# The first norm's modulation, cut from halves into quarters

## The chip, the cores and the metric

The kernel runs on one core of a Trainium2 chip. The metric is the device time of one execution in microseconds (us). A core has engines that run side by side, each through its own list of instructions in a fixed order: PE (matmuls; PEld is its weight load), DVE and POOL (vector work), ACT (activations, also copies), SP (here only DMA issue). DMA queues move data between HBM and the on-chip memory SBUF; PE writes to PSUM.

## The reference

Two layers of a diffusion backbone work on 512 latent tokens and 256 context tokens of width 1024, in 32-bit floats. What matters here is the start of layer 0:

```
def rmsnorm(x, g):
    y = xf * lax.rsqrt(jnp.mean(xf * xf, axis=-1, keepdims=True) + NORM_EPS)
    return (y * g.astype(jnp.float32)).astype(x.dtype)

def modulate(h, shift, scale):
    return h * (1 + scale) + shift
...
aq_x, bq_x, ak_x, av_x, bk_x, bv_x = jnp.split(h_x @ w_in, cuts, axis=-1)
```

`shift` and `scale` are products of a conditioning vector with a weight matrix `ada_w`: the latent tokens have one vector (`c`), the context tokens another (`c_ctx`), with the same weights. The modulated `h` then goes into a wide projection. Its first unit is two heads' K and Q and a block of V; attention on them follows, while the next unit is projected. The rest of the kernel (attention, output projection, feed-forward, layer 1) is the same in both versions.

## The kernel before

Activations lie with the feature on the partitions: `xr[k]`, k = 0 to 7, is the latent x of features 128k to 128k+127, a tile of 128 x 512; `cr[k]` is the context's, 128 x 256. `hb[k]` holds the modulated h of tile k in two parts, a rounded high part and the low rest, for latents (`hx`) and context (`hc`). A weight tile too is split: `wh` by a cast on ACT, `wl` by a subtraction on DVE. Each product is three matmuls: high x high, high weight x low h, low weight x high h.

The start of layer 0 (function `add_ada0` and the block below it) runs like this. `ada_w` for shift and scale is loaded in two halves `b`, of eight 512 KB tiles each (128 rows, 512 columns of shift and of scale). `ada0_mm(b)` multiplies them on PE with the conditioning columns, in four groups of 32 columns of the array side by side, into the PSUM tile `t`. `ada0_h(b)` copies the sums (`ada_acc`, DVE), turns them by PE transposes, adds the bias (`mod`) and makes 1 + scale times the gain (`amod`), and then makes h for four feature tiles: `h_make` multiplies x by `amod` and by x's 1/rms `ns_y` into `ns_h` (DVE), adds the shift into the high part (ACT), and makes the low part (DVE).

`part(range(4))` then runs the products of feature tiles 0 to 3 for K, Q (PSUM tiles `lin`, 512 columns) and V (`s`, 256 columns); the context's rms and its tiles 0 to 3 are made behind it in program order; the second half of the modulation follows, `part(range(4, 8))`, and context tiles 4 to 7. `keep_busy` puts matmuls of no use on PE, in waits. Behind the block, `qk_x` applies rope to K and Q (DVE and POOL) and evacuates them, `qk_c` and `v_group` project the context, and the attention steps begin; K's halves are swapped by a DMA (`k<-k`), which the second of each pair of score matmuls needs.

The code's order is not the engines' order. Tiles come from pools with a set number of buffers; a scheduler orders each engine's instructions by its own model of time, unless `tc.issue_after` sets an instruction behind another. `Stream` (`S`) holds the weight loads in order; `request` issues DMAs ahead, `next` makes the split and hands out the tile. At most eight SP loads are under way: each waits for the one eight before it on its semaphore.

## Time and profile before

| | |
|---|---|
| median of 3 runs | 1638.08 us (1630.61 to 1639.51) |
| the profiled execution, its own time | 1638.05 us |
| its span, first to last instruction | 1636.2 us |
| busy PE / DVE / ACT / POOL | 96% / 77% / 46% / 17% |
| granted clock of PE | 0.991 |
| first modulation matmul; first product | 12.94 us; 26.60 us |
| last K and Q product of latents starts | 57.76 us |
| first attention score | 79.75 us |

A row of the profile in order of time gives the start, the duration, the engine, the line of the kernel, the operation, out<-in by the program's names, the shape and a count; in brackets stands how long the engine was idle before it, and what ended that. Matmuls are pipelined, so that a row is longer than the distance to the next. In rows of stretches, the columns stand in the order that the text names.

### The profile page before, as it was taken

The numbers are of one execution on the slowest core, as the hardware profiler recorded it, in microseconds if no ns is written. First come the engines' busy times: TensorE is split into PE (matmuls) and PEld (weight loads), VectorE is DVE, ScalarE is ACT, GpSimd is POOL, SyncE is SP. The second block draws the span as 40 slices with busy tenths as digits, with TensorE's granted clock in tenths as the row PEclk, the third lists the DMA queues.
The fourth block names the chain that finished last, engine by engine and source line by source line (L and its number), as shares of the span: only waits on it lengthen the run. The fifth ranks groups of instructions, "written<-read, shape, count | busy, mean of one in ns | idle before, by whom it ended". The sixth has DMA issues, their size and how long they took to land.

```text
span 1636.2 us, 26336 instructions
## 1 busy us (share of the span) xinstructions
PE 1569.7 (96%) x10222; PEld 1404.1 (86%) x10222; DVE 1255.7 (77%) x2156; ACT 747.8 (46%) x1325; POOL 271.1 (17%) x312
## 2 busy tenths in 40 slices
PE   5999998999999899999999999999999999999997
PEld 3798987877878899999999998887788899989897
DVE  4757698976597788979898877787665987869686
ACT  4446554556344433432424254455654542524344
POOL 2222222345010000010100011264322000000001
PEclk9999999999999999999999999999999999999999
DMA  9312244544235365576766752311010442323321
GB/s 342 99 57 87 87 158 125 185 136 133 68 116 158 94 180 162 143 203 170 192 181 166 210 141 90 104 52 39 14 40 15 156 136 69 122 86 104 116 78 52
DMA packets 69364, 199.00 MB, mean 122 GB/s; under 512 B 6916, under 2 KB 19364, under 8 KB 69240
## 3 DMA queue, kind: packets, MB, share of 16 engines
q1 hardware_dynamic: 59464, 164.40, 31.2%
q0 software_dynamic: 9200, 32.39, 9.3%
q8 instruction: 81, 1.33, 0.3%
q10 hardware_dynamic: 576, 0.52, 0.1%
q14 instruction: 43, 0.35, 0.1%
HBM read 160.45 MB, written 4.86 MB: 101 GB/s over the span
## 4 chain that ended last, share of the span: by engine, by line
PE 62%; DVE 8%; DMA 4%; issue 4%; ACT 2%; POOL 0%; DVEq 0%; SPq 0%; ACTq 0%; POOLq 0%
PE f L1274 4%; PE f L1272 4%; PE f L1273 4%; PE f L1685 4%; PE f L1684 4%; PE f L1683 4%; PE f L1314 3%; PE f L1313 3%; PE f L1315 3%; PE t L1517 2%; PE lin L207 2%; PE lin L208 2%; PE lin L209 2%; DMA wl<-raw 2%; PE f L1736 2%
## 5 line engine op out<-in xcount | busy, mean ns | idle before, releaser
L196 ACT ACTIVATE wh<-raw 128x1024 fp32r<-128x1024 f32 (+1 forms) x95 | 91.2, 976 | 227.8 <-DVE raw L507 100.8
L207 PE MATMUL lin<-hb,wh 128*128 128x512 f32 (+1 forms) x456 | 163.1, 358 | 7.5 <-DVE q L372 2.2
L208 PE MATMUL lin<-hb,wh 128*128 128x512 f32 (+1 forms) x456 | 160.4, 352 | 0.1
L209 PE MATMUL lin<-hb,wl 128*128 128x512 f32 (+1 forms) x456 | 159.1, 349 | 0.0
L197 DVE TENSOR_TENSOR wl<-raw,wh 128x1024 fp32r<-128x1024 f32 (+1 forms) x95 | 105.9, 1121 | 36.3 <-ACT wh L196 34.2
L269 DVE SCALAR_TENSOR_TENSOR junk<-raw,tables 128x1024 bf16<-128x1024 f32 x80 | 98.4, 1230 | 16.8 <-DMA raw<-in_ada_wT_dram 16.4
L202 POOL DMA_DIRECT2D wl<-raw x40 | 34.9, 873 | 449.4 <-ACT wl L201 405.0
L207 PEld LDWEIGHTS lin<-hb,wh 128*128 128x128 f32 x456 | 86.6, 190 | 22.2 <-issue 4.3
L1313 PE MATMUL f<-g,wh 128*128 128x256 f32 (+1 forms) x304 | 102.7, 339 | 0.8 <-DVE s L1302 0.6
L1314 PE MATMUL f<-g,wh 128*128 128x256 f32 (+1 forms) x304 | 102.7, 339 | 0.0
L1684 PE MATMUL f<-hb,wh 128*128 128x256 f32 x360 | 101.7, 283 | 0.0
L1272 PE MATMUL f<-hb,wh 128*128 128x384 f32 x288 | 97.4, 338 | 4.4 <-ACT q L1259 4.4
L1683 PE MATMUL f<-hb,wh 128*128 128x256 f32 x360 | 101.4, 283 | 0.0
L1685 PE MATMUL f<-hb,wl 128*128 128x256 f32 x360 | 101.2, 283 | 0.0
L1315 PE MATMUL f<-g,wl 128*128 128x256 f32 (+1 forms) x304 | 100.6, 336 | 0.0
L158 ACT CAST wh<-raw 128x1024 fp32r<-128x1024 f32 x61 | 63.9, 1048 | 78.6 <-PE lin L208 24.5
L1274 PE MATMUL f<-hb,wl 128*128 128x384 f32 x288 | 97.2, 338 | 1.0 <-DMA wl<-raw 1.0
L1273 PE MATMUL f<-hb,wh 128*128 128x384 f32 x288 | 97.2, 337 | 0.0
L208 PEld LDWEIGHTS lin<-hb,wh 128*128 128x128 f32 x456 | 86.8, 190 | 11.5 <-issue 0.9
L159 DVE TENSOR_TENSOR wl<-raw,wh 128x1024 fp32r<-128x1024 f32 x61 | 79.3, 1301 | 22.2 <-ACT wh L158 22.1
L209 PEld LDWEIGHTS lin<-hb,wl 128*128 128x128 f32 x456 | 86.7, 190 | 10.5 <-issue 0.3
L339 POOL TENSOR_TENSOR ns_a<-ns_a,ns_s 128x256 f32<-128x256 f32 (+1 forms) x16 | 18.9, 1178 | 435.3 <-ACT ns_s L335 426.5
(395 smaller groups left out, 4952.6 us busy)
## 6 DMA issues: line engine op xcount, KB each, us to landing
raw<-in_w_dram SPq DMA_DIRECT2D x132, 512.0 KB, 3.6
raw<-in_ada_wT_dram SPq DMA_DIRECT2D x80, 512.0 KB, 3.8
wl<-raw POOLq DMA_DIRECT2D x40, 512.0 KB, 5.8
raw<-in_w_ab_dram SPq DMA_DIRECT2D x24, 512.0 KB, 4.1
raw<-in_ada_w_dram SPq DMA_DIRECT2D x16, 512.0 KB, 9.5
k<-k SPq DMA_DIRECT2D x16, 384.0 KB, 5.9
raw<-in_w_c_dram SPq DMA_DIRECT2D x12, 512.0 KB, 3.9
nb<-in_na_bias_dram POOLq DMA_DIRECT2D x16, 256.0 KB, 3.6
```

What stands on the lines that cost most here:

```text
L207: nc.tensor.matmul(ps, wh(k), xh(k), start=k == 0, stop=False)
L208: nc.tensor.matmul(ps, wh(k), xl(k), start=False, stop=False)
L209: end = nc.tensor.matmul(ps, wl(k), xh(k), start=False, stop=k == n - 1)
L1272: nc.tensor.matmul(ps, wh(k), b[:, 0, :], start=k == 0, stop=False)
L1273: nc.tensor.matmul(ps, wh(k), b[:, 1, :], start=False, stop=False)
L1274: nc.tensor.matmul(ps, wl(k), b[:, 0, :], start=False, stop=k == 3)
L1313: nc.tensor.matmul(ps, hi, g[:, 0, cols[v]], start=first, stop=False)
L1314: nc.tensor.matmul(ps, hi, g[:, 1, cols[v]], start=False, stop=False)
L1315: nc.tensor.matmul(ps, lo, g[:, 0, cols[v]], start=False, stop=last)
L1683: nc.tensor.matmul(ps, wh(k), b[:, 0, :], start=k == 0, stop=False)
L1684: nc.tensor.matmul(ps, wh(k), b[:, 1, :], start=False, stop=False)
L1685: nc.tensor.matmul(ps, wl(k), b[:, 0, :], start=False, stop=k == 3)
```

## The change

- `ada_w` for the first norm comes in quarters of two feature tiles. A buffer of 512 KB holds two row blocks (128 x 2 x 256 each) and is loaded by two DMAs of 256 KB. SP's first 43 DMAs are chained, so that they go in the written order; the conditioning row `crow` is loaded second, not after x.
- Per quarter there are 32 modulation matmuls of 128 columns (before, 32 of 256 for each half), one transpose, two adds and one scale.
- x/rms is made ahead by DVE (`scaled`, tiles `xn`), in buffers borrowed from the attention's pools (`Places`). h is then made by two ACT passes with the scale and the shift as operands (the high part, and a 32-bit copy) and one DVE subtraction, in place of DVE, ACT, DVE.
- The products run by feature tile: K and Q of tile k (`part_kq`), V of tile k (`part_v`). Between them stand the next quarter's modulation matmuls, half behind `part_v(k)`, half behind `part_kq(k + 1)`; `queued` fixes this.
- The context's rms comes in the last quarter, and all eight context tiles are made behind the last modulation.
- PE begins with 44 `keep_busy` matmuls; 20 stand behind the first quarter (before: 10 and 9 behind the two halves' transposes).
- The weight splits of the first unit are queued behind named instructions (`pins`); those of the second V half lie in a pool of their own.

```diff
+        def start(self, dst, src):
+            with queued(*(self.chain or [])[-1:]):
+                dma = nc.sync.dma_start(dst, src)
...
     def ada_mm(ps, raw, k, first, last):
         for j in range(4):
-            nc.tensor.matmul(
-                ps[32 * j : 32 * j + 32, 0:256], csil[:, k, :], raw[:, j * 256 : (j + 1) * 256], start=first, stop=last
-            )
...
+            end = nc.tensor.matmul(ps[32 * j : 32 * j + 32, 0:P], csil[:, k, :], raw[:, j * P : (j + 1) * P], start=first, stop=last)
+        return end
...
+            S.pools["ada"] = s0.enter_context(tc.tile_pool(name="p0_ada", bufs=6, reuse_waits="tile"))
...
+            keep_busy(psk, 44)
...
+            def ada0_h(b, ps):
+                sb = p0.tile([P, P], F32, tag="ada_acc", name="ada_acc", bufs=2)
+                nc.vector.tensor_copy(sb, ps[:, 0:P])
+                made = ada_out(sb, tp, 2 * b)
+                if b == 0:
+                    scaled((2, 3), made)
+                ends = []
+                for k in (2 * b, 2 * b + 1):
+                    t = p0.tile([P, NX], F32, tag="ns_h", name="ns_h", bufs=2)
+                    for z in (hx[k][:, 0, :], t):
+                        act = nc.scalar.activation(z, xn[k], AF.Identity, bias=mod[0][:, 0, 0, k : k + 1], scale=amod[0][:, 0, 0, k : k + 1])
+                    ends.append((act, nc.vector.tensor_sub(hx[k][:, 1, :], t, f32(hx[k][:, 0, :]))))
+                if b == 0:
+                    scaled(range(4, KT), ends[1][1])
+                return made, ends
...
+            ps = tp()
+            end = ada0_mm(ps, range(4), 16)
+            rx = rstd_of(tp(), sq_sum(xr, px, apart=True), D, px)
+            keep_busy(psk, 20, end)
+            root = rms_made[-1]
+            scaled(range(2))
+            made, ends = ada0_h(0, ps)
+            pins.extend([(root, made), (ends[0][0], ends[0][1]), ends[1]])
...
-            part(range(4))
-            rc = rstd_of(tp(), sq_sum(cr, p0), D, p1)
-            for k in range(4):
-                h_make(k, hc[k], cr[k], rc, 0, 0, 1, p0)
-            ada0_h(1, ada0_mm(1))
-            keep_busy(tp(), 9)
-            wv.append(tuple(wslice(t, 256) for t in S.next()))
-            part(range(4, KT))
-            for k in range(4, KT):
-                h_make(k, hc[k], cr[k], rc, 0, 0, 1, p0)
...
+            for b in range(1, 4):
+                k = 2 * b - 2
+                ps = tp()
+                part_kq(k)
+                ada0_mm(ps, range(2), (16, 20, 22)[b - 1], part_v(k))
+                end = ada0_mm(ps, range(2, 4), (16, 20, 22)[b - 1], part_kq(k + 1))
...
+                if b == 3:
+                    with queued(*c_pins, end):
+                        rc = rstd_of(tp(), sq_sum(cr, pc_), D, pc_)
+                part_v(k + 1)
+                _, ends = ada0_h(b, ps)
...
+            ctx_h(range(4))
+            part_kq(KT - 2)
+            part_kq(KT - 1)
+            part_v(KT - 2)
+            part_v(KT - 1)
+            ctx_h(range(4, KT))
```

What the engines get, at the places that matter. First DVE before, from the last step of x's rms (`ns_y`) to the last weight split of K, Q and V:

```order
L321 SCALAR_TENSOR_TENSOR ns_y<-ns_t,ns_y 128x512
L649 COPY ada_acc<-t 128x256
L249 TENSOR_TENSOR mod_116<-t,adab 128x2x2 x4
L257 SCALAR_TENSOR_TENSOR amod_118<-mod_116,ng 128x2x4
L353 SCALAR_TENSOR_TENSOR ns_h<-res,amod_118,ns_y 128x512 x2
L159 TENSOR_TENSOR wl<-raw,wh 128x1024
L341 TENSOR_TENSOR ns_a<-ns_a,ns_s 128x256
L355 SCALAR_TENSOR_TENSOR hb_124<-ns_h,mod_116,hb_124 128x512
L355 SCALAR_TENSOR_TENSOR hb_125<-ns_h,mod_116,hb_125 128x512
L341 TENSOR_TENSOR ns_a<-ns_a,ns_s 128x256
L353 SCALAR_TENSOR_TENSOR ns_h<-res,amod_118,ns_y 128x512
L159 TENSOR_TENSOR wl<-raw,wh 128x1024
```

And DVE after, over the same stretch (the borrowed buffers are called `scratch`; L738 is x/rms, L218 the weight split, L729 the low part):

```order
L350 SCALAR_TENSOR_TENSOR scratch<-scratch 128x512
L738 TENSOR_TENSOR scratch<-res,scratch 128x512 x2
L266 TENSOR_TENSOR mod_117<-t,adab 128x2x2 x2
L273 SCALAR_TENSOR_TENSOR amod_119<-mod_117,ng 128x2x2
L738 TENSOR_TENSOR scratch<-res,scratch 128x512 x2
L218 TENSOR_TENSOR wl<-raw,wh 128x1024
L729 TENSOR_TENSOR hb_124<-ns_h,hb_124 128x512
L729 TENSOR_TENSOR hb_125<-ns_h,hb_125 128x512
L738 TENSOR_TENSOR scratch<-res,scratch 128x512 x4
L218 TENSOR_TENSOR wl<-raw,wh 128x1024 x2
```

The x/rms of all eight tiles now stands ahead of the second and third weight split, and the context's sums are gone from here.

On PE, the turn-around from one modulation to the products that use it; before, at the second half (L235 modulation, L243 transposes, L219 fillers, L667 to L669 K and Q):

```order
L677 MATMUL s<-wl,hb_127 128x256
L235 MATMUL t<-raw,craw 32x256 x28
L243 MATMUL t<-ident,ada_acc 128x128 x2
L219 MATMUL t<-ones,ident 128x128 x9
L667 MATMUL lin<-hb_128,wh 128x512 x2
L668 MATMUL lin<-hb_128,wh 128x512
```

After, on PE at the second quarter's turn-around (L771 the last V product of tile 1, L262 the transpose, L759 to L761 K and Q, L769 V):

```order
L771 MATMUL s<-wl,hb_125 128x256
L262 MATMUL t<-ident,ada_acc 128x128
L759 MATMUL lin<-hb_126,wh 128x512 x2
L769 MATMUL s<-wh,hb_126 128x256 x2
L760 MATMUL lin<-hb_126,wh 128x512
L761 MATMUL lin<-hb_126,wl 128x512
```

There are three such places now; the modulation matmuls have moved ahead between the products, and no filler stands behind the transpose.

On PE, where the context's products end and the scores begin, before (L399 to L401 the context's V, L804 and L805 scores):

```order
L399 MATMUL lin<-wh,hb_131 128x256
L400 MATMUL lin<-wh,hb_131 128x256
L401 MATMUL lin<-wl,hb_131 128x256
L804 MATMUL s<-k_630,q 128x256
L805 MATMUL s<-k_631,q 128x256
```

And after (L229 and L230 the context's Q, L917 the first score, L428 the first of the context's V):

```order
L229 MATMUL lin<-hb_131,wh 128x256
L230 MATMUL lin<-hb_131,wl 128x256
L917 MATMUL s<-k_755,q 128x256
L428 MATMUL lin<-wh,hb_124 128x256
L429 MATMUL lin<-wh,hb_124 128x256
```

The first score has moved ahead of the context's V, and V's second half no longer lies behind the context's K and Q.

## The prediction

> **What bounds the kernel now.** I read the page's head first, then busy times by stretch, since the change touches only the start, then the start's instructions in order of time.

> ```profile
> span 1636.2 us, 26336 instructions
> ```

> ```profile
> 0.00:74.00 74.00, 52.30 (x371) 38.47 (x372) 45.09 (x84) 33.74 (x57) 22.00 (x28) 0.95 0.66 233
> 74.00:1637.00 1563.00, 1517.43 (x9854) 1365.63 (x9852) 1210.58 (x2072) 714.05 (x1268) 249.10 (x284) 0.99 0.40 116
> ```

> The columns are the stretch, its length, busy time (and instructions) of PE, PEld, DVE, ACT and POOL, the granted clock, the DMA share and GB/s. Behind 74 us PE works 97% of the time, so a delay at the start is a delay at the end unless a later wait takes it up. Before it PE stands 21.7 us. I measure the change by one mark, the first attention score with all projections of the first unit done: 79.75 us.

> ```profile
> 12.94 1.08 PE L235 MATMUL t<-raw,craw 128*32 128x256 f32 x8 [12.94 <-DMA raw<-in_ada_w_dram]
> ...
> 15.67 3.78 PE L312 MATMUL t<-ns_a,ones 128*128 128x512 f32 x4 [0.37 <-DVE ns_a L341]
> ...
> 19.38 2.37 PE L235 MATMUL t<-raw,craw 128*32 128x256 f32 x40
> ...
> 22.34 0.64 PE L235 MATMUL t<-raw,craw 128*32 128x256 f32 x8 [0.60 <-DMA raw<-in_ada_w_dram]
> ...
> 23.87 2.40 PE L219 MATMUL t<-ones,ident 128*128 128x128 f32 x20
> ...
> 26.60 0.50 PE L667 MATMUL lin<-hb,wh 128*128 128x512 f32 x1 [0.34 <-ACT hb L354]
> ...
> 28.81 0.50 PE L668 MATMUL lin<-hb,wh 128*128 128x512 f32 x1 [1.70 <-DVE hb L355]
> ...
> 73.99 0.28 PE L399 MATMUL lin<-wh,hb 128*128 128x256 f32 x1
> ...
> 79.75 0.28 PE L804 MATMUL s<-k,q 128*128 128x256 f32 x1
> ```

> A 32-bit matmul leaves two records, so x8 is four matmuls. The modulation of tiles 0 to 3 waits for its weights until 22.34; the first product (K of tile 0) runs at 26.60, and the next waits 1.70 us for the low half on DVE. From 73.99 to 79.75 run the 48 products of the context's V, 0.12 us each; those of 512 columns I take at twice that, 0.24.

> **The change part by part.** The sum is made on the profiled execution: 1638.05 us, of which 1.85 lie around the span; the median of the three runs is 1638.08.

> *To the first product.* PE now begins with 44 filler matmuls. The row at 23.87 gives ten in 2.40 us, 0.24 each. They can begin when the identity is made, at 3.5 us (POOL row below). At full rate throughout they end at 14, at half rate throughout at 24.6. In the trace PE is at half rate from 12.94 (1.08 us for what takes 0.64 at 22.34) through the sums at 15.67 and at full rate at 19.38, some 6 us later with gaps in between. I take 5 us at half rate: they end at 16.4.

> ```profile
> 3.18 0.31 POOL masks.py:199 TENSOR_SCALAR_AFFINE_SELECT ident<-ident 128x128 f32<-128x128 f32 x1
> ...
> 22.25 0.69 DVE L321 SCALAR_TENSOR_TENSOR ns_y<-ns_t,ns_y 128x512 f32<-128x512 f32 x1
> ...
> 24.47 0.17 DVE L257 SCALAR_TENSOR_TENSOR amod<-mod,ng 128x8 f32<-128x8 f32 x1
> ...
> 25.84 1.32 ACT L354 ACTIVATE hb<-ns_h,mod 128x512 fp32r<-128x512 f32 x2
> 26.01 1.22 DVE L159 TENSOR_TENSOR wl<-raw,wh 128x1024 fp32r<-128x1024 f32 x1
> ```

> ```profile
> 1091.38 1.09 PE L1517 MATMUL t<-pt,gv 128*64 128x128 f32 x16
> ```

> A quarter's modulation is 32 matmuls, 64 records of 128 columns in place of 256. With 256 columns and 32-wide weights a record takes 2.37/40, 0.056 without the tail. L1517 has 128 columns on 64-wide weights, two groups of the array side by side, and takes 0.055 a record (16 in 1.09, tail off), half of the full-width filler's 0.11. So time goes with columns and width, and I take 0.028: 2.0 us a quarter with the tail. The upper end is 0.056, 3.7 us, since no row shows a quicker matmul. The first quarter ends at 18.4. The sums of squares are three matmuls now, at full rate half of the 1.89 that each took at 15.67: 21.3. From their end to x's rms it was 3.5 us (19.45 to 22.94): 24.8. Two x/rms products (0.69 each, as at 22.25), two of the adds and the scale (0.35), one ACT pass (0.66): the first product at 27.4, 0.8 later than before. The smaller first load buys nothing, because PE is late, not the DMA. The 20 fillers end at 26.1, beside the rms.

> *Pair 0.* Behind the scale, at 26.6, DVE's order has two x/rms (1.4), a weight split (1.22), two low halves (1.4), four x/rms (2.8) and two splits (2.44): V's low weights come at 35.9. Eight V products are left on PE, and the 64 records of quarter 1 stand behind them: 38.9. PE idles behind its first product as it did at 28.81, and then the clock was halved:

> ```profile
> 30.00:32.00 2.00, 1.51 (x4) 0.66 (x2) 2.00 (x3) 1.13 (x2) 2.00 (x1) 0.50 1.04 386
> ```

> Most of that falls where DVE is late anyway; I add 0.6 (bounds 0 and 3): 39.5.

> *Turn-around and period of a quarter.* From the last record of a quarter: 12 V products (1.44), a transpose (0.4), adds and scale (0.35), one ACT pass (0.66), hops (0.2): 3.0. No filler or other product is left to put there, so PE idles 1.2 us of it. Then 4 products on the high half (0.7), 0.7 of waiting for the second ACT pass and the subtraction, and 14 products and the next quarter's records: 4 x 0.24 + 10 x 0.12 + 1.0 + 6 x 0.24 + 1.0 = 5.6. So a quarter takes 10.0, and tiles 2, 4 and 6 reach PE at 42.5, 52.5 and, with the context's sums (two matmuls of 256 columns, 0.95, and their wait), 63.5. Before, there was one turn-around behind the first. The DMAs are not late: a buffer for quarter 2 comes free when quarter 1's first tile is read, at some 38, and is needed at 47; loads of that size, x's, took 6.0 us to land:

> ```profile
> res<-in_xT_dram SPq DMA_DIRECT2D x8, 256.0 KB, 6.0
> ```

> *The tail.* The last pair has 36 products, 5.8, and 0.7 of waiting: 70. The context's K and Q (48 x 0.12) would end at 75.8, but their tiles are now all made last on DVE, where four of eight stood at 42.84 beside PE's work:

> ```profile
> 42.84 0.88 DVE L353 SCALAR_TENSOR_TENSOR ns_h<-res,amod,ns_y 128x256 f32<-128x256 f32 x2
> ...
> 59.35 2.33 DVE L353 SCALAR_TENSOR_TENSOR ns_h<-res,amod,ns_y 128x256 f32<-128x256 f32 x2
> ...
> 64.00 2.33 DVE L372 SCALAR_TENSOR_TENSOR k<-rbuf,k 64x512 fp32r<-64x512 f32 x2
> 66.36 2.21 DVE L159 TENSOR_TENSOR wl<-raw,wh 128x1024 fp32r<-128x1024 f32 x1
> ```

> From 64.2 DVE has two low halves (1.4), eight context tiles (8 x 0.9), four rope operations (2.8) and the K and Q low parts (2.8): 78.4. Beside POOL's rope work the same shapes took 1.45, about 0.95 and 0.99 us more (59.35 to 66.36), 3.4 in all; I take 2 (bounds 0 and 3.4): 80.4, and PE ends K and Q 0.5 later. Then one cast (1.05), one split (1.22) and K's context low part (0.88) stand ahead of the first score, which PE's order now has ahead of the V products: 84.1. Then 48 V products, 5.8: 89.9 in place of 79.75. Before, the second V half, 48 products, lay over that evacuation; now it is spent. Costed at nothing: x/rms itself (one DVE pass replaces one, ACT's 8 extra passes of 0.66 are in the turn-around), the earlier table load (hidden before the x tiles), lambda's few small operations (beside quarter 2's products).

> The sum is 10 us: 1648.

> [...] The row at 28.81 shows the clock halved after a gap of 1.70 us. [...]

> **The rivals.**

> *Modulation at 0.056, or half clock in each turn-around.* The first costs 1.7 us in each of four quarters: 7, so 1655. The second costs some 3.5 us in three turn-arounds: 1658. [...]

> *The delay is taken up later (not slower).* The order also shifts in the heads of about 240 to 440 us, where PE stands:

> ```profile
> 220.00:240.00 20.00, 17.78 (x114) 15.48 (x113) 19.12 (x30) 10.86 (x23) 4.03 (x2) 1.00 0.38 128
> 240.00:260.00 20.00, 16.16 (x95) 12.94 (x93) 17.45 (x31) 11.40 (x25) 2.72 (x2) 1.00 0.37 120
> ```

> If the new order closed these 6.1 us, 1642; with the like behind them, 1636. It decides from 2 us on, where the loss falls under 8. Against it: DVE is 87 to 96% busy there, and gets no less work.

> *Faster.* If DVE kept ahead of PE, the products (24 us), three quarters (6), sums (1) and the context (12) from 27.4 on would end at 70, ten before 79.75: 1628. Against it stands DVE's order in pair 0 and in the tail.

> **How the numbers follow.** The forecast (1643 to 1653) gets 0.5, the dearer cases 0.2, the delay taken up 0.19, faster 0.11. A measurement of this kernel tells about 0.5%, 8 us, from no change: of the forecast 0.1 lies under 8, so slower 0.6, same 0.29, faster 0.11. The range runs from 1634, into the case taken up, to 1661, past the dearer ones; the forecast's own is 1643 to 1653.

> **What the profile after would show.** First product at 27 to 28; a modulation record at 0.028; PE waiting twice at each of three turn-arounds; the first score waiting on DVE's K part, ahead of the context's V; that V ending near 90; PE's idle before 90 over 21 us. I am wrong if that V ends before 82, or if it ends near 90 and the span is not 6 us longer.

## The result, and the profile after

The changed kernel takes 1663.49 us (median of four runs, 1658.61 to 1666.81) against 1637.27 for the kernel before: ratio 1.0168, interval 1.0141 to 1.0194. It is 26 us slower. The forecast was slower by 10, with a range up to 1661: the sign was right, the time lies outside. The profiled execution, the longest of the four, took 1666.81 us; 1.81 of them lie around its span. A second set of five runs gave 1659.4 us against 1633.33, ratio 1.0153 (1.0133 to 1.0174).

The page's head, then busy times by stretch (columns as in the prediction):

```profile
span 1665.0 us, 26804 instructions
```

```profile
0.00:74.00 74.00, 58.41 (x543) 48.85 (x544) 30.84 (x67) 32.34 (x51) 10.37 (x19) 0.95 0.66 219
74.00:1665.00 1591.00, 1533.57 (x9900) 1377.63 (x9899) 1224.62 (x2093) 721.38 (x1282) 255.83 (x294) 0.99 0.40 115
```

The first row misleads: PE is busier there than before (58.41 against 52.30 us), but 64 filler matmuls are in it, against 19 before. The second stretch is 28 us longer than before, so most of the loss shows only behind 74 us. The start in order of time on PE (L240 and L238 fillers, L256 modulation, L341 sums, L262 transpose, L759 and L760 K of tile 0):

```profile
11.83 4.18 PE L240 MATMUL lin<-ones,ident 128*128 128x128 f32 x36
15.94 1.52 PE L256 MATMUL t<-raw,craw 128*32 128x128 f32 x48
17.96 0.43 PE L256 MATMUL t<-raw,craw 128*32 128x128 f32 x8 [0.49 <-DMA raw<-in_ada_w_dram]
20.57 0.43 PE L256 MATMUL t<-raw,craw 128*32 128x128 f32 x8 [2.19 <-DMA raw<-in_ada_w_dram]
20.92 2.84 PE L341 MATMUL t<-scratch,ones 128*128 128x512 f32 x6
23.60 4.63 PE L238 MATMUL lin<-ones,ident 128*128 128x128 f32 x40
28.07 0.27 PE L262 MATMUL t<-ident,ada_acc 128*128 128x128 f32 x1
29.83 0.50 PE L759 MATMUL lin<-hb,wh 128*128 128x512 f32 x1 [1.50 <-ACT hb L728]
31.92 0.50 PE L760 MATMUL lin<-hb,wh 128*128 128x512 f32 x1 [1.59 <-DVE hb L729]
```

The fillers end at 16.0, close to the forecast 16.4, and PE then waits for the last loads until 20.57: the DMA was late, not PE. Since the sums stand behind the modulation, the whole rms follows that load. The three turn-arounds:

```profile
43.56 0.73 PE L759 MATMUL lin<-hb,wh 128*128 128x512 f32 x2 [1.36 <-ACT hb L728]
45.00 0.50 PE L760 MATMUL lin<-hb,wh 128*128 128x512 f32 x1 [0.47 <-DVE hb L729]
54.08 0.73 PE L759 MATMUL lin<-hb,wh 128*128 128x512 f32 x2 [1.36 <-ACT hb L728]
55.51 0.50 PE L760 MATMUL lin<-hb,wh 128*128 128x512 f32 x1 [0.47 <-DVE hb L729]
66.96 0.73 PE L759 MATMUL lin<-hb,wh 128*128 128x512 f32 x2 [1.37 <-ACT hb L728]
68.39 0.50 PE L760 MATMUL lin<-hb,wh 128*128 128x512 f32 x1 [0.47 <-DVE hb L729]
```

Two waits at each, of the size forecast. The end of the start, first DVE's list, then PE (L229 the context's Q, L917 and L918 scores, L428 to L430 the context's V), then the clock by stretches:

```profile
78.03 1.16 DVE L382 SCALAR_TENSOR_TENSOR ns_h<-res,amod,scratch 128x256 f32<-128x256 f32 x1
79.11 1.51 DVE L384 SCALAR_TENSOR_TENSOR hb<-ns_h,mod,hb 128x256 fp32r<-128x256 f32 x1
...
84.45 0.48 DVE L384 SCALAR_TENSOR_TENSOR hb<-ns_h,mod,hb 128x256 fp32r<-128x256 f32 x1
86.68 1.23 DVE L171 TENSOR_TENSOR wl<-raw,wh 128x1024 fp32r<-128x1024 f32 x1 [1.75 <-ACT wh L170]
87.94 0.87 DVE L401 SCALAR_TENSOR_TENSOR k<-lin,k 64x256 fp32r<-64x256 f32 x2
```

```profile
83.03 0.39 PE L229 MATMUL lin<-hb,wh 128*128 128x256 f32 x1 [1.37 <-DVE hb L384]
...
84.99 0.58 PE L229 MATMUL lin<-hb,wh 128*128 128x256 f32 x1 [0.79 <-DVE hb L384]
...
88.41 0.58 PE L917 MATMUL s<-k,q 128*128 128x256 f32 x1 [2.20 <-DVE k L401]
88.96 0.55 PE L428 MATMUL lin<-wh,hb 128*128 128x256 f32 x1
89.31 0.41 PE L429 MATMUL lin<-wh,hb 128*128 128x256 f32 x1
...
96.83 0.28 PE L430 MATMUL lin<-wl,hb 128*128 128x256 f32 x1
97.32 0.39 PE L918 MATMUL s<-k,q 128*128 128x256 f32 x1 [0.21 <-DMA k<-k]
```

```profile
83.70:88.40 4.70, 1.72 (x7) 1.13 (x5) 2.83 (x5) 3.13 (x5) 0.00 (x0) 0.50 0.00 0
90.00:94.00 4.00, 4.00 (x21) 4.00 (x21) 0.91 (x3) 0.00 (x0) 0.00 (x0) 0.51 1.02 232
```

PE waits for DVE's context tiles; behind these waits of 0.3 to 1.4 us the clock is at half from 83.7 on, so already ahead of the longest wait, the 2.20 us for K's low part (the L229 row at 84.99 takes 0.58, the one at 83.03 0.39). The context's V then runs at 0.21 us a product until 94 and at 0.12 behind that. The second score row stands at 97.32, where before it stood at 79.87.

How the delay of one instruction grows, each time against the same instruction of the kernel before (start times; the lines are those of before):

| instruction, and its time before | after | delay |
|---|---|---|
| first product, 26.60 | 29.83 | 3.2 |
| second score row (L805), 79.87 | 97.32 | 17.5 |
| first context scores (L769), 119.49 | 137.05 | 17.6 |
| last context attention (L852), 287.88 | 302.02 | 14.1 |
| last head's V products (L982), 444.69 | 469.20 | 24.5 |
| first feed-forward product (L1272), 557.12 | 586.17 | 29.1 |
| end of the span, 1636.2 | 1665.0 | 28.8 |

So there are two losses: 17.5 us in the start, and some 7 from 119 to 445 us, where only the order of the engines differs. What follows behind 445 us scatters. In the second profile of the same kernel the delays at 119 us, at 445 us and at the end were 19.0, 24.4 and 17.0: the wait of 6.64 us ahead of the first feed-forward product, shown further down, was not there.

### The profile page after: what moved, and what is told of

Read it like the earlier page. It is cut to its first block, busy times and chain, and to the rows that moved or that the text cites. A ratio compares the mean times of both kernels' runs of the same rounds, so it can differ in the third digit from the quotient of the medians.

```text
span 1665.0 us, 26804 instructions
## 1 busy us (share of the span) xinstructions
PE 1592.0 (96%) x10442; PEld 1426.5 (86%) x10442; DVE 1255.5 (75%) x2159; ACT 753.7 (45%) x1333; POOL 266.2 (16%) x312
## 4 chain that ended last, share of the span: by engine, by line
PE 51%; DVE 6%; DMA 5%; issue 5%; ACT 2%; POOL 0%; DVEq 0%; POOLq 0%; ACTq 0%; SPq 0%
PE f L1799 4%; PE f L1798 4%; PE f L1797 4%; DMA wl<-raw 3%; PE f L1388 3%; PE f L1386 3%; PE f L1387 3%; PE f L1428 3%; PE f L1427 3%; PE f L1429 3%; PE t L1631 2%; PE f L1851 2%; PE f L1852 2%; PE f L1850 2%; PE t L1617 2%
## 5 line engine op out<-in xcount | busy, mean ns | idle before, releaser
L217 ACT ACTIVATE wh<-raw 128x1024 fp32r<-128x1024 f32 (+1 forms) x99 | 95.2, 979 | 232.1 <-DVE raw L536 124.5
L229 PE MATMUL lin<-hb,wh 128*128 128x512 f32 (+1 forms) x456 | 161.4, 354 | 3.9 <-DVE hb L384 3.6
L230 PE MATMUL lin<-hb,wl 128*128 128x512 f32 (+1 forms) x456 | 160.1, 351 | 0.0
L218 DVE TENSOR_TENSOR wl<-raw,wh 128x1024 fp32r<-128x1024 f32 (+1 forms) x99 | 110.4, 1122 | 35.2 <-ACT wh L217 32.9
L228 PEld LDWEIGHTS lin<-hb,wh 128*128 128x128 f32 x456 | 87.0, 192 | 23.5 <-issue 7.8
L229 PEld LDWEIGHTS lin<-hb,wh 128*128 128x128 f32 x456 | 87.2, 191 | 16.8 <-DVE hb L384 4.7
L1388 PE MATMUL f<-hb,wl 128*128 128x384 f32 x288 | 97.5, 338 | 0.1
L230 PEld LDWEIGHTS lin<-hb,wl 128*128 128x128 f32 x456 | 87.1, 191 | 10.8 <-issue 0.7
L170 ACT CAST wh<-raw 128x1024 fp32r<-128x1024 f32 x57 | 59.7, 1047 | 79.4 <-PE lin L229 25.9
L171 DVE TENSOR_TENSOR wl<-raw,wh 128x1024 fp32r<-128x1024 f32 x57 | 73.7, 1294 | 25.6 <-ACT wh L170 25.3
L368 POOL TENSOR_TENSOR ns_a<-ns_a,ns_s 128x256 f32<-128x256 f32 (+1 forms) x12 | 12.4, 1037 | 427.1 <-ACT ns_s L364 420.5
## 6 DMA issues: line engine op xcount, KB each, us to landing
raw<-in_ada_w_dram SPq DMA_DIRECT2D x32, 256.0 KB, 5.7
nb<-in_na_bias_dram POOLq DMA_DIRECT2D x16, 256.0 KB, 3.3
```

The source lines that it names most:

```text
L228: nc.tensor.matmul(ps, wh(k), xh(k), start=k == 0, stop=False)
L229: nc.tensor.matmul(ps, wh(k), xl(k), start=False, stop=False)
L230: end = nc.tensor.matmul(ps, wl(k), xh(k), start=False, stop=k == n - 1)
L1388: nc.tensor.matmul(ps, wl(k), b[:, 0, :], start=False, stop=k == 3)
```

## The experiments

Each kernel was timed beside the kernel before, whose median was then 1632.67 to 1633.58 us. They ran on four chips, so between kernels of different rounds the ratios, with their 95% intervals, are the safer comparison. The base of most is the changed kernel with 52 fillers, the first one below. The delay at the first context scores (119.49 us before) and at the last head's V (444.69) is given as in the table, against the profile of before. That profile is itself some 1 to 1.7 us late there: in the four kernels that alter it only further on, the row at 59.49 us came 1.0 to 1.7 us earlier.

**The order between 240 and 440 us.** The scheduler's order there flips with a few fillers. So four fillers can give the kernel before the order of after, and eight can give the changed kernel the order of before, with nothing else moved.

```diff
-            keep_busy(psk, 44)
+            keep_busy(psk, 52)
```

> The changed kernel with 52 instead of 44 fillers ahead of the first modulation. The eight more end some 1.9 us later, still before the last load of the first quarter (20.57 us), so the start should stand as it is; but with them the order of the engines between 240 and 440 us is that of the kernel before. Theory O (the changed order between 240 and 440 us costs the 7 us by which the offset grows there): about 7 us less than the changed kernel, 1656.5. Rival D (the order costs nothing; a late start is what makes those stages wait longer): 1663, within 2 us.

```diff
-        ps = linp().rearrange("p (t c) -> p t c", t=2)
+        ps = linp()
+        keep_busy(ps, 4, c_end[0])
+        ps = ps.rearrange("p (t c) -> p t c", t=2)
         v_group(ps, 0, wv)
```

`c_end` is the last product of the context's Q. With four fillers the order of after results on PE, row for row, with 80 that of before, with six a third.

> The kernel before with four fillers (0.24 us each) ahead of the context's V. They alone make the order between 240 and 440 us that of the changed kernel, row for row. Theory O: 1 us for the fillers and 7 for the order, 1645. Rival D: 1 us for the fillers, 1638.

> The kernel before with 80 fillers at that place, some 19 us of pure delay of PE, as much as the changed kernel is late at its first scores (17.5 us); the order between 240 and 440 us stays that of the kernel before. Theory O: the delay goes through to the end one for one, 1655 to 1657. Rival D: it grows on the way as in the changed kernel (17.5 to 26), 1664. A third way, that later waits take part of it up: below 1650.

> The kernel before with six fillers (1.4 us) at that place: a third order between 240 and 440 us, unlike both. Theory O: 1639 for the fillers alone, and by the order some us more or less, of unknown sign; a time below 1637 would be a better order than both. Rival D: 1638.5, within 2 us.

> The changed kernel as it is, on the chip on which the variants ran, as a reference for them and for the waits behind 440 us. Theory O (the order between 240 and 440 us costs 4 to 7 us): 1660 to 1664, that is 4 to 7 us over the kernel with 52 fillers (1656.6). Rival D: 1656 to 1658, the same as that kernel. Behind 440 us, if the wait of the last output-projection load (2 us) belongs to this start, it shows again at 2 us; if it is chance, at 0.8 to 1.2.

| kernel | median, us | ratio (interval) | delay at 119 / 445 us |
|---|---|---|---|
| after, again | 1659.4 | 1.0153 (1.0133 to 1.0174) | 19.0 / 24.4 |
| after, 52 fillers | 1656.63 | 1.0138 (1.0123 to 1.0154) | 17.7 / 18.8 |
| before, 4 fillers | 1638.16 | 1.0021 (1.0007 to 1.0034) | -0.3 / 3.7 |
| before, 6 fillers | 1635.89 | 1.0009 (0.9994 to 1.0024) | 0.3 / 1.0 |
| before, 80 fillers | 1651.53 | 1.0105 (1.0090 to 1.0119) | 16.2 / 14.0 |

The same stretch of work, from the last context attention to the last head's V, first in the kernel before, then after, then with 52 fillers, then before with four and with 80:

```profile
287.88:444.69 156.81, 152.24 (x1087) 126.94 (x1085) 113.53 (x208) 79.65 (x184) 57.81 (x82) 1.00 0.43 134
```

```profile
302.02:469.20 167.18, 157.90 (x1098) 130.54 (x1096) 115.89 (x210) 80.19 (x184) 56.72 (x82) 0.98 0.42 126
```

```profile
305.33:463.51 158.18, 153.19 (x1087) 127.26 (x1085) 112.44 (x208) 79.69 (x184) 56.37 (x82) 1.00 0.44 133
```

```profile
285.40:448.38 162.98, 156.46 (x1097) 129.19 (x1095) 115.41 (x210) 79.97 (x184) 57.30 (x82) 0.99 0.44 129
```

```profile
301.06:458.69 157.63, 152.67 (x1088) 126.91 (x1086) 114.13 (x208) 79.40 (x184) 59.23 (x82) 1.00 0.44 133
```

With the order of after the stretch takes 163 to 167 us, with that of before 157 to 161 over all profiles, however late it begins. Part of that is gained back ahead of it: from 119 to 288 us the delay falls by 2 to 4 us with the order of after (17.6 to 14.1 in after). From 119 to 445 us together the delay grows by 4.0 to 6.9 us in the three profiles with the order of after, and by -2.2 to 3.5 in fifteen profiles of altered kernels with that of before. Theory O holds in kind. By whole times the order is worth less: the two ratios of after (1.0168 and 1.0153) lie 1.4 to 3.0 thousandths over the two with 52 fillers (1.0138, and 1.0139 when run again), and four fillers cost the kernel before 2.1, of which the fillers themselves are 0.6. That makes 2 to 5 us. The intervals of these ratios overlap, so it is the profiles that show the loss, and its size is not sure. In the two kernels with the order of after PE waits for the same thing in the middle of the stretch, a low part of Q on DVE, and in after also for K's swap DMA:

```profile
352.26 0.47 PE L228 MATMUL lin<-hb,wh 128*128 128x512 f32 x1 [1.84 <-DVE q L401]
...
406.30 0.36 PE L1025 MATMUL s<-k,q 128*128 128x256 f32 x1 [1.83 <-DMA k<-k]
```

```profile
333.33 0.47 PE L207 MATMUL lin<-hb,wh 128*128 128x512 f32 x1 [1.82 <-DVE q L373]
```

The 80 fillers took 18.02 us in the trace and came out as 17 us by the ratio, 18.0 by the medians: a delay at the start goes through one for one. D's growth with lateness is excluded.

**The first product.** First the weight loads were to be held back, then the sums were put ahead of the modulation.

```diff
-            with queued(*(self.chain or [])[-1:]):
+            with queued(*(self.chain or [])[-1:], *self.gate):
...
+                    S.gate = [end] if first and t == 2 else []
```

> The changed kernel with 52 fillers (so that the order between 240 and 440 us is that of the kernel before; the base, 1656.6), in which the three first weight loads (512 KB each) are held until six of the eight modulation loads of the first quarter have been used. Theory W (these weights share the DMA engines with the last modulation loads, which therefore land at 19.2 to 20.6 us in place of about 18): first product 1 to 2 us earlier, at 27 to 27.5. Rival (the modulation loads are late by their own bytes): first product at 28.5 to 29.8 as before. For the time, theory P (PE and DVE take the whole start as one chain, so 1.5 us gained there are 1.5 us at the end): 1655; rival (the gain is lost in the first pair, where PE waits for weight splits): 1656.6.

The last modulation load was used at 19.56 (19.22 in the base), the first product came at 28.83 (28.49), and the time was 1657.26 (1.0151, 1.0128 to 1.0174). But the edit did not hold the loads. SP's rows with the three weight loads, in the base and in this kernel:

```profile
13.00 1.85 SPq L138 DMA_DIRECT2D raw<-in_w_ab_dram  x3
```

```profile
13.07 1.59 SPq L139 DMA_DIRECT2D raw<-in_w_ab_dram  x3
```

SP issued them at the same time in both, while PE's first modulation matmul ran only at 17.23: the gate names a matmul on PE, and the DMA on SP did not wait for it. So this run tests neither theory W nor its rival, and why the last load comes as late as 19 to 21 us is open.

```diff
+            rx = rstd_of(tp(), sq_sum(xr, px, apart=True), D, px)
             end = ada0_mm(ps, range(4), 16)
-            rx = rstd_of(tp(), sq_sum(xr, px, apart=True), D, px)
-            keep_busy(psk, 20, end)
+            keep_busy(psk, 6, end)
```

> The changed kernel with the sums of squares of x put on PE ahead of the first quarter's modulation (as in the kernel before), 40 fillers ahead and 6 behind in place of 44 and 20; the order between 240 and 440 us is that of the kernel before. Theory S (in the changed kernel x's rms runs after the last modulation load has landed, 3 sums and 3.5 us of rms on the path, where before it was hidden): first product at 24 in place of 28.5 to 29.8, the first scores 4 us earlier, 1652. Rival (DVE's list in the first pair, x/rms and the splits, takes it up): first product at 24, the scores at most 1.5 us earlier, 1655.

```profile
13.98 2.74 PE L341 MATMUL t<-scratch,ones 128*128 128x512 f32 x6
...
19.36 0.43 PE L256 MATMUL t<-raw,craw 128*32 128x128 f32 x8 [0.34 <-DMA raw<-in_ada_w_dram]
...
23.90 0.80 PE L759 MATMUL lin<-hb,wh 128*128 128x512 f32 x1 [2.48 <-ACT hb L728]
```

The fillers ahead are 40 here. The rms now runs while the loads come, and the first product stands at 23.90, 2.7 us ahead of the kernel before and 4.6 ahead of the base, although the last load was used no earlier (19.36). The delay at 119 us fell from 17.7 to 9.1, the time to 1645.47 (1.0087, 1.0066 to 1.0108), 8 us under the base by the ratio and 11 by the medians: twice what theory S said. The 4.6 us at the first product are the place of the sums; the other 4 us arose further on, 1.5 of them in a quarter in which the base's clock was halved, and the rest was not traced.

**The turn-arounds and the clock.**

```diff
+        turn = nc.tensor.transpose(pt[:, 0:P], sb, ident)
+        if k0:
+            keep_busy(psum(), 9, turn)
...
+        keep_busy(tp(), 10, c_end[0])
```

> The changed kernel with 48 fillers at the start (same order between 240 and 440 us as the base), nine more behind each of the three later transposes and ten ahead of the first score. Theory H (the halved clock behind the waits at the turn-arounds and at the end costs some 2 us there and 2.5 in the context's V): 1652, and the context's V at 0.12 us each throughout. Rival (what is lost to the clock is hidden by DVE and ACT, which set the turn-arounds): V quicker by 2.5 us at most and the turn-arounds as they were, 1654; or no gain at all, 1656.6.

```profile
40.00:50.00 10.00, 9.90 (x139) 8.85 (x132) 3.85 (x10) 4.09 (x6) 0.00 (x0) 0.99 0.75 234
50.00:60.00 10.00, 9.92 (x119) 8.42 (x117) 2.96 (x8) 5.20 (x11) 0.86 (x2) 1.00 0.98 345
86.00:90.00 4.00, 3.57 (x29) 3.21 (x28) 3.75 (x6) 2.54 (x6) 0.00 (x0) 1.00 0.40 81
```

The clock stays full, and the transposes of the last three quarters stood at 43.08, 53.61 and 64.99, 10.5 and 11.4 us apart. In the base they were 12.1 and 11.4 apart (40.56, 52.63, 64.03), in after 10.5 and 12.9 (41.93, 52.45, 65.32), the clock being halved for a part of the 12.1 and of the 12.9. So at full clock a quarter takes 10.5 us, 11.4 with the context's sums, and a halved clock adds 1.5 where it falls. Fillers take nothing off the 10.5: PE's waits there are for ACT and DVE. More came at the end: the second score row stands at 94.22 in place of 97.61, the delay at 119 us is 15.4, the time 1651.98 (1.0115, 1.0096 to 1.0134). Then the way of making h, undone (the x/rms tiles go as well):

```diff
-                    for z in (hx[k][:, 0, :], t):
-                        act = nc.scalar.activation(z, xn[k], AF.Identity, bias=..., scale=...)
-                    ends.append((act, nc.vector.tensor_sub(hx[k][:, 1, :], t, f32(hx[k][:, 0, :]))))
+                    h_make(k, hx[k], xr[k], rx, 0, 0, 0, p0)
```

> The changed kernel with h made as before, by DVE, ACT and DVE, without the x/rms tiles and the second ACT pass (44 fillers; the order between 240 and 440 us is that of the kernel before). Theory N (this way of making h is neutral; the quarters and the tail cost the time): within 1.5 us of 1656.6. Rival X (the x/rms of eight tiles ahead of the splits in the first pair, and ACT's second pass of 0.72 us ahead of each low half, cost 1 us in each of four quarters): 1652.5.

1647.82 (1.0088, 1.0069 to 1.0108), 9 us under the base; but the quarters were as long as the others at full clock, 10.6 and 11.4 (transposes at 43.52, 54.10, 65.54), and the delay at 119 us was 16.7, 1 less. So X's mechanism is not what happened. Both kernels were run again side by side:

> The changed kernel with 52 fillers once more (1656.6 and 1.0138 the first time), beside the next, to see whether the 9 us between the two return. Both have the same instructions in the same order behind the start. If the difference belongs to the kernels: 1656 to 1658. If it is scatter between executions that the intervals do not show: anywhere from 1650 to 1658, and the ratio of the two within 0.3%.

> The changed kernel with h made as before (DVE, ACT, DVE) once more (1647.8 and 1.0088 the first time). If the 9 us belong to it: 1647 to 1649. If to chance: 1651 to 1656, 1 to 3 us under the other, as its first scores show.

1658.47 (1.0139, 1.0111 to 1.0167) and 1652.69 (1.0113, 1.0088 to 1.0138): 6 us, with intervals that overlap, and of the 6.4 us between their profiles 2.7 show at 119 us. The rest arose behind 445 us, 3 of it at two waits for transfers. PE's row where the output projection waits for the last load (the row names DVE, but ACT had waited 3.24 us for that load's landing to make its `wh`), and the first feed-forward product, in after, and then with h made as before (first time):

```profile
488.68 0.47 PE L228 MATMUL lin<-hb,wh 128*128 128x512 f32 x1 [2.01 <-DVE res L1181]
...
586.17 0.69 PE L1386 MATMUL f<-hb,wh 128*128 128x384 f32 x1 [6.64 <-ACT q L1373]
```

```profile
480.59 0.47 PE L228 MATMUL lin<-hb,wh 128*128 128x512 f32 x1 [1.24 <-DVE res L1174]
...
571.87 0.44 PE L1379 MATMUL f<-hb,wh 128*128 128x384 f32 x1 [1.52 <-ACT q L1366]
```

The second wait ran from nothing to 6.6 us over the profiles, and the clock was already at half behind those of 4.32, 4.41 and 6.64 us (0.69 for the same matmul, in place of 0.44 behind 1.91, 1.52 and 0.77). It does not belong to a kernel: in after it was 6.64 and, the second time, nothing. With this h it was short twice (1.52 and 1.91) and 5.10 in the last variant below; what sets it is open.

**The tail.** The context's tiles made earlier, and then, alone, the context's V in another PSUM pool:

```diff
-                if b == 3:
+                if b == 2:
                     with queued(*c_pins, end):
                         rc = rstd_of(tp(), sq_sum(cr, pc_), D, pc_)
...
-            ctx_h(range(4))
+                if b == 2:
+                    ctx_h(range(4))
```

> The base with the context's rms in the third quarter and context tiles 0 to 3 made ahead of the last quarter, in place of all eight behind the last modulation. Theory T (DVE's list at the end of the start sets the first score: eight context tiles, ropes and low parts): four tiles less, some 4 to 5 us earlier: first score at 84, the context's V done by 92, 1652. Rival (the four tiles delay the last quarter by as much, or the end hangs on PE, POOL's rope work and the clock): within 1.5 us of 1656.6.

1653.53 (1.0121, 1.0100 to 1.0143). Theory T in part: the delay at 119 us fell by 6 to 11.5, but half came back by 445 us (14.7); PE's order there is that of the kernel before, and the cause is open.

```diff
-        ps = linp().rearrange("p (t c) -> p t c", t=2)
+        ps = tp((P, 2, 256))
         v_group(ps, 0, wv)
```

> The changed kernel (46 fillers; order between 240 and 440 us as before) with one thing altered: the context's V goes into a PSUM tile of the transposes' pool, so that its products no longer stand behind the first score. Theory V (the tail is the step that was priced too low: waits of 8 us on DVE's context tiles with nothing else to run, then V at halved clock): the V products fall into those waits, the first scores come 6 to 8 us earlier than at 97.5 us, 1649. Rival (the context's tiles are ready too late for V to fill anything): 2 to 3 us, 1654.

PE from 74 to 86 us, in after, and with this one line:

```profile
74.00:86.00 12.00, 7.83 (x48) 6.43 (x47) 10.70 (x16) 5.80 (x11) 4.55 (x5) 0.90 0.00 0
```

```profile
74.00:86.00 12.00, 10.56 (x79) 9.73 (x79) 11.45 (x16) 8.66 (x16) 4.79 (x6) 1.00 0.09 15
```

V fills the waits, the clock stays full, the delay at 119 us is 6.5 in place of 17.7, and the time 1647.88 (1.0083, 1.0061 to 1.0105), 9 us under the base. Theory V holds. The first two score rows themselves came only 3.5 and 4.3 us earlier (85.10 and 93.29), because products of the next unit now stand between them; the whole gain shows further on. In the kernel before the same line brought nothing:

> The kernel before with the same one alteration; its order puts 12 of the context's V products into the second half's turn-around and the second half of them behind the context's K and Q. If such cover is worth time there too: the waits of 0.6 to 1.3 us between 49 and 69 us (3.7 us in all) shrink, 1630. If it is not (V already ran without a wait, and its place behind K and Q covered the evacuation): 1633, within 2 us.

1631.87 (0.9993, 0.9980 to 1.0006): its V had cover enough.

**All together.** Sums ahead and context early, with the edit on the weight loads too; then V's place as well; then that with fillers, and with h made as before. The weight loads are held in none of the four: SP issued them at 13.2 to 13.7 us. So these are two and three edits that act, not three and four.

> The sums ahead, the three weight loads held, and the context's rms and tiles 0 to 3 ahead of the last quarter, all in one; order between 240 and 440 us as before. If these three add up (4, 1 and 4 to 6 us at the first scores): 1646. If DVE is then the bound from the first pair to the end, so that only the context's part counts: 1652.

> As the last, and the context's V goes into a PSUM tile of another pool (the transposes'), so that it need not wait for K's evacuation: PE's order now has 13 of its products in the last turn-around and the rest among the context's K and Q, and its second half behind them, over the evacuation. Theory V (the context's V spent behind the evacuation is 5 to 6 us of the loss, the step on the tail): 1640, near the kernel before; PE's waits between 60 and 90 us under 4 us in all. Rival (the first score waits on DVE's list all the same): the V is done earlier but the first score comes as late, 1645.

> The last variant (sums ahead, weights held, context's tiles early, context's V in the transposes' pool) with nine fillers behind each of the four transposes and three behind the first modulation. Theory H (half clock behind the waits of 2.4, 1.6 and 1.4 us): no row of K and Q at 0.43 us a step between 24 and 60 us, 2 to 4 us less, 1631. Rival (DVE and ACT set these places): 1634, within 2 us.

> The same variant with h made as before (DVE, ACT, DVE) and without x/rms. The changed kernel with h made so was 9 us quicker by the medians, of which its first scores showed 1. If the rest belongs to that way of making h: 1626 to 1628. If it was a matter of loads and waits behind 440 us in that kernel alone: first scores within 1 us of the variant without it, 1633 to 1634.

| kernel | median, us | ratio (interval) | delay at 119 / 445 us |
|---|---|---|---|
| sums ahead, context early | 1641.12 | 1.0057 (1.0034 to 1.0079) | 3.8 / 2.8 |
| and V's place | 1634.08 | 1.0012 (0.9996 to 1.0028) | -0.8 / -2.1 |
| that, with fillers | 1639.91 | 1.0036 (1.0020 to 1.0052) | -0.9 / -1.3 |
| that, h as before | 1634.36 | 1.0007 (0.9990 to 1.0025) | 1.1 / -0.7 |

With the three edits the quarters equal the kernel before; no version of them was faster than it. So the 17.7 us of the start are accounted for by the place of the sums, of the context's tiles and of the context's V. One at a time these took 8.6, 6.2 and 11.2 us off the delay at 119 us, 26 in all: they overlap, and the single gains do not add up. With the fillers the median is 6 us higher, and the profile can't say why: it is of the shortest of their twelve runs (1633.56 us), and its start is no later than without them.

## Why the prediction was right or wrong

| step | forecast, us | measured |
|---|---|---|
| fillers end | 16.4 | 16.0 |
| a quarter's modulation, tail in | 2.0 | 1.95 |
| first product | 27.4 | 29.83 |
| tiles 2, 4, 6 reach PE | 42.5, 52.5, 63.5 | 43.56, 54.08, 66.96 |
| last pair done on PE | 70 | 73.5 |
| context tiles done on DVE | 80.4 | 84.9 |
| first score | 84.1 | 88.41 |
| context's V done | 89.9 | 97.0 |
| added behind | 0 | 7 in the profile, 2 to 5 by ratios |

*Right:* the direction; the price of a modulation record (64 in 1.95 us, 0.03 each and not 0.056); two waits at each turn-around; the first score on K's low part, ahead of V; and that a delay at the start is a delay at the end (80 fillers).

*Where the sum failed.* The start was priced at 10 us and cost 17 (V's end at 97.0 in place of 89.9), and a term put at nothing, the order behind the start, cost 2 to 5 more. Step by step the start's 7 us are 2.4 to the first product, -1.4 in the first pair, 2.4 in the quarters, 1.0 in the context's tiles, -0.2 in K's evacuation and 2.8 in V. Of the 26 us by the medians some 2 to 6 remain; they arose behind 445 us and are open.

*To the first product.* "The smaller first load buys nothing, because PE is late, not the DMA" failed. I let PE's sums follow the modulation at 18.4, without asking when the last of the 256 KB loads lands: it was used at 20.57. In the kernel before the first half, twice the bytes, was used at 22.34, only 1.8 us later. That the sums and the rms follow this load was in my sum; what I passed over is that the change itself put them there. The row at 15.67, quoted in the prediction, shows the sums ahead of the last modulation, where they cost the path nothing, and putting them back there was worth 8 to 11 us.

*The first pair* hid a part of this by luck: from the first product to tile 2 I had 15.1 us, measured were 13.7. DVE's list behind the scale took 8.4 us (28.93 to 37.30) where I had 9.3, mostly because the x/rms products stand 0.61 apart, priced at 0.7.

*Turn-around and period of a quarter.* 10.5 where I had 10.0, and 12.9 for the quarter with the context's sums, where I had 11.0. The two waits were right (1.36 and 0.47 us, forecast 1.2 and 0.7); where the 0.5 lies is not shown, and with h made as before a quarter took 10.6 too. Of the 12.9, 1.5 are the halved clock, which I had weighed as a rival and thought unlikely: it came in one turn-around of three, not in all (the clock, below).

*The tail* is the term of the start that was mis-sized most: from the last pair to the end of V I had 19.9 us, measured were 23.5. DVE's list was only slightly longer; V, priced at 5.8 us at full clock, took 8.0 (88.96 to 97.0), because the clock stood at half until 94. It had fallen at 83.7 already, behind PE's short waits for the context's tiles. And the 20 us were no fact of DVE: V could have run inside them in a PSUM tile of another pool than K's, which one line showed (9 us).

*The delay is taken up later.* I used the changed order between 240 and 440 us only as a rival that gains. It lost, by 4 to 7 us in the profiles and 2 to 5 by the ratios. I had no row from which to read that sign; a term of 0 with a range to both sides belonged in the sum.

*The clock at the turn-arounds.* The sum prices them at full clock, with gaps of 1.2 and 0.7 us. That was my estimate; no row that it quotes shows it. The gaps came out as 1.36 and 0.47 us, and the clock stayed full around one turn-around and fell around the next:

```profile
40.00:50.00 10.00, 8.16 (x92) 6.38 (x85) 3.85 (x10) 4.09 (x6) 0.00 (x0) 1.00 0.89 278
50.00:60.00 10.00, 8.17 (x87) 6.95 (x91) 3.78 (x10) 5.71 (x12) 1.46 (x2) 0.83 0.85 301
```

The rows are ten microseconds around the first and around the second turn-around: the same gaps, the same busy time, and a granted clock of 1.00 once and 0.83 the next time; with 52 fillers it was the other way round (0.83, then 1.00). In after the clock changed at 32.45, 35.86, 56.34, 59.76, 83.65 and 93.89 us, always whole multiples of 3.41 us apart. Counted from 32.45 in steps of 3.41 us, one step ends at 46.10, where the clock stayed, and one at 56.34, where it fell:

```profile
42.69:46.10 3.41, 2.07 (x9) 1.60 (x10) 1.13 (x2) 3.40 (x5) 0.00 (x0) 1.00 0.93 251
52.93:56.34 3.41, 1.79 (x8) 1.37 (x9) 1.06 (x4) 3.12 (x5) 0.00 (x0) 1.00 1.07 389
```

## What to carry to other kernels

When a stage is cut finer, ask for each wait that is left what else PE may run there, and what keeps it from running: here a PSUM pool (9 us) and the place of three matmuls (8 to 11 us) each cost about half a per cent, and with both mended the cut still brought nothing. Before pricing a smaller load, ask when it lands. Before reading an experiment, look in its trace whether the edit did what it was for: the loads meant to be held went out at the same time as ever. Where a scheduler orders the whole program, an edit can flip an order hundreds of us away, and a few fillers flip it back: hold that order fixed before crediting a difference of half a per cent to the edit.

## What the hardware showed beyond that

- An ACT pass of 128x512 with the scale and the shift as operands took 0.80 us, one behind the other 0.71 apart; with the shift alone, in the kernel before, a pass took 0.71 us and two together 1.32 (priced at 0.66 each):

```profile
42.70 0.81 ACT L728 ACTIVATE hb<-scratch,mod,amod 128x512 fp32r<-128x512 f32 x1 [8.90 <-DVE amod L273]
43.42 0.80 ACT L728 ACTIVATE ns_h<-scratch,mod,amod 128x512 f32<-128x512 f32 x1
```

- The last load of the output projection, 512 KB with next to nothing else under way (0.53 to 0.55 MB were moved in each of those stretches), was ready for its use 3.4 us after its issue in before and 3.8 with h as before, but 4.6 us in after and 4.7 with 52 fillers; run again, these three gave 4.0, 4.5 and 4.7. The instructions there are the same; the cause is open.
